# Second feed-forward product of a transformer block: two groups side by side through the seven products, sums and casts in a fixed order, token blocks of the output projection in another order

## The chip, the cores and the metric

One core of one Trainium2 chip. The number is device microseconds (us) of one execution of the whole program. A trace's own span (first to last instruction) is a little shorter than the time of the execution that was profiled.

## The reference, cut to what matters

512 tokens, model width 1024, feed-forward width 4096. After attention, mLSTM and their gates, the block ends in

```python
h = layer_norm(DEEPNORM_ALPHA * h + merged @ w_out[l], ln1_g[l], ln1_b[l])
ff = jnp.square(jax.nn.relu(h @ w_ff1[l])) @ w_ff2[l]
r = DEEPNORM_ALPHA * h + ff
r = r + jax.nn.sigmoid(r @ w_ple_gate[l]) * (p[l] @ w_ple_proj[l])
h = layer_norm(r, ln2_g[l], ln2_b[l])
```

All of it is fp32 in and out.

## The kernel before, in words

**Three matmuls for one.** Every fp32 operand is split into a rounded fp32r part and the rest (`split`, L105 to L107: ACT casts `hi`, DVE or POOL subtracts to get `lo`), and each product is hi·hi + hi·lo + lo·hi (`mm3`, L132 to L135). So each weight and each activation passes once through ACT and once through DVE or POOL before TensorE (PE) sees it.

**Seven products for eight.** Both feed-forward products are done as Winograd's variant of Strassen's: a 2x2 block product with seven block products, whose operands are sums of blocks.

**First feed-forward product** (`ff1`, L862): 16 column pieces of w_ff1, each with seven 256-wide products; `left_factors` (L786) loads a piece, POOL makes the four sums (`sums`, L793 to L796), ACT and DVE split. The other operand, `hcH`/`hcL`, holds seven combinations of the transposed first layer norm's output; `h_factors(i)` (L738) makes them of token block i: the transposes `hps` on PE, then copies, sums and splits on ACT and DVE. Blocks 0 and 1 give the plain combinations HB11 and HB21, blocks 2 and 3 all the others.

**What stands ahead of it.** The output projection (`out_projection(i, hh)`, L810: 24 matmuls for token block i and column half hh, then a DVE op adds into `r`), the first norm of each block (`first_norm`, `layer_norm` L699; its power on POOL is L705, its last two DVE operations are L715 and L716), and eight small products of the `p` input (`ple_projection`, six matmuls each, tile `ppw`).

**Second feed-forward product** (L888 to L1036). The 4096 rows of w_ff2 are four groups g. A group's activations are four blocks a11, a21, a12, a22 (two tiles `uL`, `uH`; those of groups 2 and 3 are spilled to DRAM during the first product, L932, and read back, L950), its weights four quarters B11, B12, B21, B22 of 1 MB each. The combined weights are made by DMAs that add while they write: `add` (L904) issues one from POOL's queue, onto a quarter `b` that SP's queue loaded (`load`, L898). Three quarters are loaded and four adds made per group: B12 and then B22 and then B21 onto B11's tile, B12 onto B22's tile. Each add waits until the splits of the tile's former content are done, and the next split of that tile waits for the add. POOL makes the activation sums `s` and those in `uL`, `uH` (L963 to L973). One product of one group is a step of 24 matmuls of 512 columns: PE goes through group 0's seven products, then group 1's, and so on (`steps`, 28 steps); `operands` makes a step's factors `wh`, `wl` (128x2048) and `ah`, `al` (128x1024), each with two buffers, while the step before runs. In a step all matmuls of one token half come first, with wh·ah, wl·ah, wh·al in turn. Products 0, 1 and 4 are kept in PSUM over all groups; the other four are added into `r` after every step (L1032, L1034).

**Behind it.** `load_gate` loads and splits w_ple_gate (`wpg`), `gate_inputs` transposes `r` (`rps`), `gate_product` makes eight gate products (`pg`), and `second_norm` finishes a block and stores it.

The order of instructions on each engine is set by a scheduler with a cost model of its own at build time; `tc.issue_after(x)` puts what is built inside it behind x.

Of the kernel before, what the change touches and what calls it, by code (L numbers as in the profile page):

```python
# [14 lines left out]
P = 128  # L15
# [40 lines left out]
def block_kernel(ctx: ExitStack, tc: tile.TileContext, t, out):  # L56
# [43 lines left out]
    def gtile(name, dtype=F32R):  # L100

        return gpool.tile([P, 4, S], dtype, tag="g", bufs=4, name=name)
# [593 lines left out]

    def layer_norm(pl, src, dst, g, b, done=None, pieces=2, cut=D):
# [6 lines left out]
        ve.tensor_scalar(ag[:, 2:3], ag[:, 1:2], EPS, None, op0=OP.add)  # L704
        ge.tensor_tensor(out=ag[:, 3:4], in0=ag[:, 2:3], in1=mhalf[:, 0:1], op=OP.pow)  # L705
# [26 lines left out]

    def h_factors(i):
# [25 lines left out]
        ve.tensor_sub(v3, hb[1][:, :, o], v2)  # L759
# [26 lines left out]
    def left_factors(q, half):  # L786
# [12 lines left out]
        for o, src in ((slice(0, 2), raw[:, :, :, 0:P]), (2, a22), (slice(3, 7), sums)):  # L799
            split(src, hi[:, o], lo[:, o], ge if q == order[0] and o != 2 and o.start == 0 else ve)  # L800
# [17 lines left out]
    for i in range(NT - 1):  # L818
        out_projection(i, 0)
    for i in range(NT - 1):  # L820
        out_projection(i, 1)
        first_norm(i)
        if i > 0:
            h_factors(i - 1)
# [5 lines left out]
    factors = [left_factors(order[0], half) for half in range(2)]  # L830
    first_norm(NT - 1)
    h_factors(NT - 2)
# [17 lines left out]
    for _ in range(2):  # L850
        ple_projection(*todo.pop(0))
# [10 lines left out]
    def ff1(q, acts):  # L862
# [6 lines left out]
        for half, (wh, wl) in enumerate(ws):  # L869
            for n, (a, b) in enumerate(pairs_):  # L870
                for c in range(2):
                    k = half * 2 + c
                    mm3(ps[n], wh[:, a, c], wl[:, a, c], hcH[:, b, k], hcL[:, b, k], k == 0, k == 3)
# [17 lines left out]

    ff2_rows = w_ff2.rearrange("(q j p) c -> j p q c", j=2, p=P)
# [5 lines left out]
    def load(g, w):  # L898
        if g < GROUPS:
            tl = place("b", [P, 4, 512], F32, g % 2 if w == B11 else 2 if w == B22 else 3)  # L900
            loads.append(sy.dma_start(tl, rows_of(g, w)))
            quarters.setdefault(g, {})[w] = tl
# [12 lines left out]
    def group_acts(g):  # L915
        acts[g] = gtile("uL", F32), gtile("uH", F32)
        return [a.rearrange("p (a b) (c q) -> p a (b c) q", a=2, c=2) for a in acts[g]]

    views = {}
    quarters = {}  # L920
    B = B11, B22, B21
    for n, q in enumerate(order):
        g = q // 4
        if q % 4 == 0:
            views[g] = group_acts(g)
        ff1(q, views[g])
        if n == 0:
            for a in todo:
                ple_projection(*a)
        if n in (5, 9):  # L930
            for c in range(2):
                sy.dma_start(spilled[order[n - 2] // 4][:, c], views[order[n - 2] // 4][c])  # L932
        if 6 <= n < 9:
            with tc.issue_after(loads[-1].ins):
                load(0, B[n - 6])
        if n == 9:
            f1, close_f1 = open_pool("f1", side="right")
            begun = [factor(f1, quarters[0][B11], "w", 512, hi=place("wh", [P, 4, 512], F32R, 1))]
            add(0, quarters[0][B11], B12)
        if n == 12:  # L940
            begun.append(factor(f1, views[0][0][:, 0], "a", 256))
# [4 lines left out]
    def load_acts(g):  # L946
        if g in spilled:
            views[g] = group_acts(g)
            for c in range(2):
                sy.dma_start(views[g][c], spilled[g][:, c])  # L950

    def ff2_steps(g):

        (a11, a21), (a12, a22) = ([v[:, 0], v[:, 1]] for v in views[g])
        b11, b22, b21 = (quarters[g][w] for w in B)
        fac = lambda a, b: (factor(late, b, "w", 512, 2), factor(late, a, "a", 256, 2))
        if g == 0:
            yield begun
        else:
            yield fac(a11, b11)  # L960
            add(g, b11, B12)
        s1 = late.tile([P, 4, 256], F32, tag="s1", bufs=1, name="s1")
        ge.tensor_sub(s1, a21, a22)  # L963
        load_acts(g + 1)
        yield fac(a12, b21)
        load(g + 1, B11)
        s3, s2 = a21, late.tile([P, 4, 256], F32, tag="s2", bufs=1, name="s2")
        ge.tensor_sub(s2, s1, a11)
        ge.tensor_add(a12, a12, s2)
        yield fac(s1, b11)  # L970
        add(g, b11, B22)
        load(g + 1, B21)
        ge.tensor_sub(s3, a11, s3)  # L973
        yield fac(a12, b22)
        add(g, b22, B12)
        yield fac(s2, b11)
        add(g, b11, B21)
        yield fac(s3, b22)
        load(g + 1, B22)
        yield fac(a22, b11)  # L980


    GATE_STEPS = (2, 2), (2, 6), (3, 1), (3, 3)
    steps = [(g, n) for g in range(GROUPS) for n in range(7)]
# [171 lines left out]
```

## Time and profile before

| | |
|---|---|
| runs (us) | 857.41, 854.6, 855.33; median 855.33 |
| the profiled execution's own time | 856.99 us |
| its span in the trace | 855.3 us |
| mean granted TensorE clock in it | 0.978 of full speed |
| busy: PE, DVE, ACT, POOL | 794.0, 645.9, 421.0, 380.4 us |
| matmul instructions | 4374 |
| moved by DMA | 104.16 MB |

A profile's busy time of an engine is the time in which it ran an instruction; an idle stretch is put down to what the instruction after it waited for. Matmuls are pipelined, so one that is shown as 0.40 us long is followed by the next one after 0.23 us; distances between starts tell the pace.

### The profile page before, as it was taken

The page shows a single profiled execution, that of the slowest core. Times are in us where ns is not written, and L with a number is a line of the kernel's source. Part 1 is how long each engine was busy: PE and PEld are TensorE (multiplying, and loading weights), DVE is VectorE, ACT ScalarE, POOL GpSimd, SP SyncE. Part 2 cuts the span into 40 slices and gives each one's busy share as a digit, 9 for nine tenths or more (in the row PEclk, how much of TensorE's full clock was granted, in tenths as well). Part 3 has the DMA queues.
Part 4 walks back from the last instruction along what each step waited for, and adds up shares of the span by engine and source line. Part 5 has one row for each costly group of instructions (what it writes and reads, how often), then busy time and mean ns, then how long its engine had stood idle before and what let it go on. Part 6 is the DMA issues. An engine that isn't in the chain of part 4 may idle for free.

```text
span 855.3 us, 11843 instructions
## 1 busy us (share of the span) xinstructions
PE 794.0 (93%) x4374; PEld 676.7 (79%) x4374; DVE 645.9 (76%) x1061; ACT 421.0 (49%) x687; POOL 380.4 (44%) x289
## 2 busy tenths in 40 slices
PE   8999999999999999999889999999779878788996
PEld 7787778779978888778689999999567656576785
DVE  5779999955469985767867898896858568587557
ACT  4445456677665633332546666665444344365110
POOL 4542443232344435461556678773825216123501
PEclk9999999999999999999989999999999999899999
DMA  7432224121132012670523786330595977958101
GB/s 214 129 94 73 57 68 110 50 72 54 51 98 74 26 50 85 209 223 26 183 81 106 245 234 223 114 99 1 148 252 142 185 208 168 275 130 165 50 25 74
DMA packets 86036, 104.16 MB, mean 122 GB/s; under 512 B 6229, under 2 KB 58965, under 8 KB 84698
## 3 DMA queue, kind: packets, MB, share of 16 engines
q1 hardware_dynamic: 76938, 84.53, 31.1%
q0 software_dynamic: 8448, 16.78, 11.5%
q10 hardware_dynamic: 592, 2.10, 0.7%
q8 instruction: 34, 0.56, 0.3%
q14 instruction: 24, 0.20, 0.1%
HBM read 95.00 MB, written 8.39 MB: 121 GB/s over the span
## 4 chain that ended last, share of the span: by engine, by line
PE 61%; DVE 18%; DMA 10%; issue 4%; ACT 3%; POOL 3%; SPq 0%; DVEq 0%; ACTq 0%; POOLq 0%
PE pf L134 8%; PE pf L135 8%; PE pf L133 8%; DMA b<-in_w_ff 8%; DVE wl L107 3%; PE pg L134 3%; PE pg L135 3%; PE pg L133 3%; DVE sc L329 2%; PE po L135 1%; PE po L133 1%; PE po L134 1%; DVE sc L339 1%; PE pu L133 1%; DVE al L107 1%
## 5 line engine op out<-in xcount | busy, mean ns | idle before, releaser
L133 PE MATMUL pf<-hcH,w1h 128*128 128x256 f32 x448 | 123.0, 285 | 5.3 <-DVE hcL L107 5.3
L134 PE MATMUL pf<-hcL,w1h 128*128 128x256 f32 x448 | 124.3, 283 | 0.0
L135 PE MATMUL pf<-hcH,w1l 128*128 128x256 f32 x448 | 118.7, 283 | 0.0
L134 PE MATMUL pf<-wl,ah 128*128 128x512 f32 x224 | 94.0, 420 | 21.7 <-DVE wl L107 21.7
L107 DVE TENSOR_TENSOR wl<-b,wh 128x2048 fp32r<-128x2048 f32 x28 | 82.8, 2956 | 32.3 <-ACT wh L106 32.3
L133 PE MATMUL pf<-wh,ah 128*128 128x512 f32 x224 | 90.0, 410 | 8.5 <-ACT wh L106 7.7
L135 PE MATMUL pf<-wh,al 128*128 128x512 f32 x224 | 91.8, 411 | 4.0 <-DVE al L107 4.0
L133 PEld LDWEIGHTS pf<-hcH,w1h 128*128 128x128 f32 x448 | 84.7, 191 | 5.8 <-DVE hcL L107 5.5
L134 PEld LDWEIGHTS pf<-hcL,w1h 128*128 128x128 f32 x448 | 85.5, 191 | 0.1
L135 PEld LDWEIGHTS pf<-hcH,w1l 128*128 128x128 f32 x448 | 82.1, 191 | 0.2 <-DVE w1l L107 0.2
L106 ACT CAST wh<-b 128x2048 fp32r<-128x2048 f32 x28 | 53.3, 1902 | 44.2 <-DMA b<-in_w_ff 40.3
L134 PEld LDWEIGHTS pf<-wl,ah 128*128 128x128 f32 x224 | 44.5, 199 | 37.8 <-DVE wl L107 28.6
L126 POOL TENSOR_TENSOR wgl<-wgr,wgh 128x1024 fp32r<-128x1024 f32 x16 | 39.4, 2464 | 66.7 <-ACT wgh L125 52.5
L107 DVE TENSOR_TENSOR w1l<-w1r,w1h 128x256 fp32r<-128x256 f32 (+1 forms) x62 | 49.0, 815 | 19.1 <-ACT w1h L106 19.1
L133 PEld LDWEIGHTS pf<-wh,ah 128*128 128x128 f32 x224 | 44.6, 199 | 20.8 <-ACT wh L106 9.7
L135 PEld LDWEIGHTS pf<-wh,al 128*128 128x128 f32 x224 | 44.9, 200 | 14.0 <-DVE al L107 4.9
L905 POOL DMA_DIRECT2D b<-in_w_ff x16 | 20.7, 1294 | 77.7 <-DVE wl L107 77.7
L134 PE MATMUL pg<-xL,wgh 128*128 128x512 f32 x128 | 51.5, 402 | 0.0
L133 PE MATMUL pg<-xH,wgh 128*128 128x512 f32 x128 | 51.4, 401 | 0.0
L135 PE MATMUL pg<-xH,wgl 128*128 128x512 f32 x128 | 51.3, 400 | 0.0
L106 ACT CAST w1h<-w1r 128x512 fp32r<-128x512 f32 x64 | 29.6, 511 | 42.7 <-PE pf L134 35.9
L793 POOL TENSOR_TENSOR sums<-w1r 128x256 f32<-128x256 f32 x32 | 25.2, 789 | 52.6 <-DVE w1l L107 44.4
(356 smaller groups left out, 2298.4 us busy)
## 6 DMA issues: line engine op xcount, KB each, us to landing
w1r<-in_w_ff SPq DMA_DIRECT2D x64, 256.0 KB, 3.1
b<-in_w_ff POOLq DMA_DIRECT2D x16, 1024.0 KB, 8.6
b<-in_w_ff SPq DMA_DIRECT2D x12, 1024.0 KB, 6.9
wgr<-in_w_in SPq DMA_DIRECT2D x16, 512.0 KB, 3.9
wor<-in_w_out SPq DMA_DIRECT2D x8, 512.0 KB, 3.9
wpgr<-in_w_ple_gate SPq DMA_DIRECT2D x8, 512.0 KB, 9.6
xrs<-in_x SPq DMA_DIRECT2D x4, 512.0 KB, 4.7
iqwr<-in_w_in SPq DMA_DIRECT2D x4, 512.0 KB, 4.9
```

What stands on the lines that cost most here:

```text
L106: se.copy(hi, src)
L107: (lo_eng or ve).tensor_sub(lo, src, f(hi))
L126: (lo_eng or ge).tensor_sub(lo, raw, f(hi))
L133: te.matmul(ps, sh, mh, start=first, stop=False, **kw)
L134: te.matmul(ps, sh, ml, start=False, stop=False, **kw)
L135: return te.matmul(ps, sl, mh, start=False, stop=last, **kw)
L329: ve.scalar_tensor_tensor(sc, rl, wi[:, i, h:h + 1], sc, op0=OP.mult, op1=OP.add)
L339: ve.match_replace(out=sc, in_to_replace=m8, in_values=sc, imm_value=NEG_TAKEN)
L793: ge.tensor_add(sums[:, 0], a21, a22)
L905: return ge.dma_start(out=tl, in_=rows_of(g, w), accum_op=OP.add)
```

## The change

1. **Two groups side by side.** `steps` now goes through pairs of groups (d = 0: groups 0 and 1; d = 1: groups 2 and 3), each step being one product of one group e of the pair. A product of both groups is summed in PSUM, and goes into `r` once per pair (`ff2_sums`).
2. **One add less per group.** The operand of P4, formerly B11's tile after its third add, is now B21's tile plus B11's tile after its second add, made on chip by DVE (`T4`).
3. **Activation sums from POOL to DVE**, ten of sixteen; six stay on POOL (`ON_POOL`).
4. **Fixed order.** `queued` chains all casts on ACT and all sums, splits and adds into `r` on DVE in the order of the program; PE's matmuls are chained too. Within a step the four wh·ah matmuls of a token half come first, then wh·al, and wl·ah of both halves last.
5. **Loads.** Only B11 of groups 0 and 1 is loaded during the first product; B21 and B22 of both follow at the first step of the second. B21 has tiles of its own. POOL's space for DMA descriptors goes from 8192 to 2048 bytes per partition. The raw gate weights are loaded some steps ahead of their splits.
6. **Ahead of the first product**: token blocks in the order 0, 2, 1, 3; the splits and sums of the first w_ff1 piece are put behind the last first norm's statistics and power, the splits of its sums behind the last block's combinations; all eight `ple_projection` come before the first product instead of six; and in its first piece the two products that need only blocks 0 and 1 (HB11, HB21) come first.

The core of the diff:

```diff
-        for o, src in ((slice(0, 2), raw[:, :, :, 0:P]), (2, a22), (slice(3, 7), sums)):
-            split(src, hi[:, o], lo[:, o], ge if q == order[0] and o != 2 and o.start == 0 else ve)
+        for o, src in ((slice(0, 2), raw[:, :, :, 0:P]), (2, a22)):
+            split(src, hi[:, o], lo[:, o], ge if q == order[0] and o != 2 else ve)
+        if later is None:
+            split(sums, hi[:, 3:7], lo[:, 3:7])
+        else:
+            later.append((sums, hi[:, 3:7], lo[:, 3:7]))
...
-    factors = [left_factors(order[0], half) for half in range(2)]
     first_norm(NT - 1)
-    h_factors(NT - 2)
+    later = []
+    with tc.issue_after(norm[0].ins), tc.issue_after(norm[1].ins):
+        factors = [left_factors(order[0], half, later) for half in range(2)]
+    h_factors(1)
...
     h_factors(NT - 1)
-    for _ in range(2):
+    with tc.issue_after(last_block[0].ins):
+        for a in later:
+            split(*a)
+    for _ in range(4):
         ple_projection(*todo.pop(0))
...
+        parts = [(half, n) for half in range(2) for n in range(7)]
+        if q == order[0]:
+            parts.sort(key=lambda x: x[1] not in (0, 4))
...
+    steps = [(0, P1, 0), (0, P5, 0), (0, P1, 1), (0, P2, 0), (0, P2, 1), (0, P5, 1)]
+    steps += [(0, P6, 0), (0, P3, 0), (0, P3, 1), (0, P6, 1), (0, P7, 0), (0, P7, 1)]
+    steps += [(1, P1, 0), (0, P4, 0), (0, P4, 1), (1, P1, 1), (1, P5, 0), (1, P5, 1), (1, P2, 0), (1, P2, 1)]
+    steps += [(1, P6, 0), (1, P3, 0), (1, P3, 1), (1, P6, 1), (1, P7, 0), (1, P7, 1), (1, P4, 0), (1, P4, 1)]
...
+    def factor_of(src, kind, width):
+        hi, lo = (late.tile([P, 4, width], F32R, tag=kind + x, bufs=2, name=kind + x) for x in "hl")
+        queued(se, "copy", hi, src)
+        queued(ve, "tensor_sub", lo, src, f(hi))
+        return hi, lo
...
+        if n == P1 and g > 0:
             add(g, b11, B12)
...
+        elif n == P5:
+            add(g, b11, B22)
+        elif n == P3:
+            add(g, b22, B12)
+        elif n == P7:
+            load(g + 2, B22)
+            load_acts(g + 2, 0)
+        elif n == P4:
+            load(g + 2, B21)
+            load_acts(g + 2, 1)
...
+        o, x, y = {"S1": (sums, a21, a22), "S2": (sums, sums, a11), "S3": (a21, a11, a21), "S4": (a12, a12, sums),
+                   "T4": (b21, b21, b11)}[which]
+        queued(engine, "tensor_sub" if which < "S4" else "tensor_add", o, x, y)
...
+        for s, kind in ((0, 0), (0, 1), (1, 0), (1, 1), (0, 2), (1, 2)):
+            tok = slice(s * P, (s + 1) * P)
+            def product():
+                for q in range(4):
+                    mm = te.matmul(bank(d, n, s), (al if kind == 1 else ah)[:, q, tok], (wl if kind == 2 else wh)[:, q],
+                                   start=fresh and kind == 0 and q == 0, stop=kind == 2 and q == 3, skip_group_check=True)
```

What it makes of the engines' orders, at the three places that matter. Numbers behind a name tell buffers apart.

POOL, before, from the first sum of the second product's group 0 on (`s`, `uL`, `uH`: activation sums; `DMA b`: an adding DMA):

```order
L963 TENSOR_TENSOR s_6602<-uL,uH 128x1024
L968 TENSOR_TENSOR s_6646<-s_6602,uL 128x1024
L973 TENSOR_TENSOR uL<-uL 128x1024
L969 TENSOR_TENSOR uH<-uH,s_6646 128x1024
L905 DMA b<-in_w_ff 128x4x512
L963 TENSOR_TENSOR s_6858<-uL,uH 128x1024
L973 TENSOR_TENSOR uL<-uL 128x1024
L905 DMA b<-in_w_ff 128x4x512
```

and after the change, the same stretch and on to the last add:

```order
L992 TENSOR_TENSOR uLH<-uLH 128x1024
L932 DMA b<-in_w_ff 128x4x512 x2
L990 TENSOR_TENSOR uLH<-uLH 128x1024
L932 DMA b<-in_w_ff 128x4x512 x6
L990 TENSOR_TENSOR s<-s,uLH 128x1024
L932 DMA b<-in_w_ff 128x4x512
L990 TENSOR_TENSOR uH<-uH,s 128x1024
L990 TENSOR_TENSOR uLH<-uLH 128x1024 x2
L932 DMA b<-in_w_ff 128x4x512 x2
```

POOL keeps six sums and eleven adds in this stretch; before, sixteen sums and fifteen adds stood there.

DVE, before, in the same place (`al`, `wl`: splits; `r`: a product added into the result):

```order
L107 TENSOR_TENSOR wl<-b,wh 128x2048
L107 TENSOR_TENSOR al<-uH,ah 128x1024
L107 TENSOR_TENSOR wl<-b,wh 128x2048
L107 TENSOR_TENSOR al<-s_6602,ah 128x1024
L107 TENSOR_TENSOR al<-uH,ah 128x1024
L1032 SCALAR_TENSOR_TENSOR r<-r,pf_6600 128x512
L107 TENSOR_TENSOR wl<-b,wh 128x2048
```

and after the change:

```order
L992 TENSOR_TENSOR s<-uLH,uH 128x1024
L990 TENSOR_TENSOR al<-s,ah 128x1024
L990 TENSOR_TENSOR wl<-b,wh 128x2048
L990 TENSOR_TENSOR al<-uLH,ah 128x1024
L990 TENSOR_TENSOR wl<-b,wh 128x2048
L990 TENSOR_TENSOR s<-s,uLH 128x1024
L990 TENSOR_TENSOR al<-uH,ah 128x1024
L990 TENSOR_TENSOR wl<-b,wh 128x2048
L990 TENSOR_TENSOR s<-uLH,uH 128x1024
```

The activation sums now stand in DVE's queue between the pairs of splits. From the first sum to the last `wl` of the stage this queue holds 27 `al`, 27 `wl`, 10 activation sums of 128x1024, 4 `T4` of 128x2048, 24 additions of a product (22 into `r`, 2 into `e`), 2 gate splits and 3 splits of `rps`.

POOL around the last first norm, before (`lag<-lag,mhalf` is the norm's power):

```order
L107 TENSOR_TENSOR w1l<-w1r,w1h 128x512
L795 TENSOR_TENSOR sums<-sums,w1r 128x256
L107 TENSOR_TENSOR w1l<-w1r,w1h 128x512
L795 TENSOR_TENSOR sums<-sums,w1r 128x256
L705 TENSOR_TENSOR lag<-lag,mhalf 128x1
```

and after the change:

```order
L112 TENSOR_TENSOR wp<-wpr,wp 128x1024
L712 TENSOR_TENSOR lag<-lag,mhalf 128x1
L802 TENSOR_TENSOR sums<-w1r 128x256
L803 TENSOR_TENSOR sums<-w1r 128x256
L112 TENSOR_TENSOR w1l<-w1r,w1h 128x512
```

The power now stands ahead of all work on the first w_ff1 piece.

## Rows read from the trace of the kernel before

**Rows 1.** The profile page: busy time of each engine with its share of the span; then the granted TensorE clock in tenths of full speed, over 40 slices of 21.4 us each.

```profile
PE 794.0 (93%) x4374; PEld 676.7 (79%) x4374; DVE 645.9 (76%) x1061; ACT 421.0 (49%) x687; POOL 380.4 (44%) x289
...
PEclk9999999999999999999989999999999999899999
```

**Rows 2.** The same engines over the second feed-forward product in four stretches: length, then busy us and count of PE, PEld (weight loads), DVE, ACT, POOL, then the granted clock, the DMA share and GB/s.

```profile
593.80:639.80 46.00, 36.34 (x148) 28.09 (x147) 32.84 (x20) 21.87 (x17) 28.32 (x10) 0.96 0.71 183
639.80:691.80 52.00, 43.24 (x169) 33.28 (x169) 34.68 (x23) 20.05 (x15) 16.55 (x8) 0.93 0.75 182
691.80:743.50 51.70, 41.80 (x169) 32.18 (x170) 36.61 (x23) 21.11 (x16) 19.01 (x9) 0.96 0.82 205
743.50:793.75 50.25, 44.33 (x171) 34.57 (x172) 41.78 (x32) 24.77 (x22) 18.34 (x10) 0.91 0.68 146
```

**Rows 3.** PE's groups of instructions from 595 to 800 us (the three kinds of matmul of the second product): busy us and mean ns | idle us ahead of them and what ended it.

```profile
L134 PE MATMUL pf<-wl,ah 128*128 128x512 f32 x217 | 91.2, 421 | 21.7 <-DVE wl L107 21.7
L135 PE MATMUL pf<-wh,al 128*128 128x512 f32 x217 | 89.1, 411 | 4.0 <-DVE al L107 4.0
L133 PE MATMUL pf<-wh,ah 128*128 128x512 f32 x217 | 87.3, 410 | 8.5 <-ACT wh L106 7.7 <-DVE r L1034 0.8
```

**Rows 4.** The chain of work that ended last, from 560 us on: shares by line, and two of its pieces (start us, length us, what).

```profile
by line: DMA b<-in_w_ff 21.8%; DVE wl L107 9.0%; PE pf L134 8.8%; PE pf L135 8.5%; PE pf L133 8.3%; issue 8.1%; PE pg L133 4.6%; PE pg L134 4.6%; PE pg L135 4.6%; DVE al L107 3.3%; ACT wh L106 3.2%; POOL r L1024 3.0%; POOL uL L973 1.8%; POO
...
623.93 11.21 DMA b<-in_w_ff
...
726.43 12.44 DMA b<-in_w_ff
```

**Rows 5.** PE in order of time: start us, length us, line, operation, and in brackets the idle time ahead and who ended it. The first two are of the first step, the next three of a later one, the last is the first matmul behind the second product.

```profile
594.03 0.40 PE L134 MATMUL pf<-wl,ah 128*128 128x512 f32 x1
...
598.81 0.39 PE L134 MATMUL pf<-wl,ah 128*128 128x512 f32 x1
...
609.72 0.79 PE L135 MATMUL pf<-wh,al 128*128 128x512 f32 x1 [2.41 <-DVE al L107]
610.31 0.63 PE L133 MATMUL pf<-wh,ah 128*128 128x512 f32 x1
...
612.87 0.41 PE L133 MATMUL pf<-wh,ah 128*128 128x512 f32 x1
...
806.13 0.39 PE L133 MATMUL pg<-wpg,rH 128*128 128x512 f32 x1
```

**Rows 6.** Who waited for whom from 594 to 806 us: total us, times, longest us.

```profile
ACT wh L106 <- DMA b<-in_w_ff: 40.0, 11, 6.7
...
DVE wl L107 <- ACT wh L106: 32.3, 16, 5.0
...
DVE al L107 <- ACT ah L106: 4.5, 7, 2.7
```

**Rows 7.** DVE in order of time, the same columns as rows 5: one `wl` beside work on POOL, then `wl`, `r`, `al`, `wl` with POOL idle.

```profile
601.87 4.49 DVE L107 TENSOR_TENSOR wl<-b,wh 128x2048 fp32r<-128x2048 f32 x1
...
637.18 2.29 DVE L107 TENSOR_TENSOR wl<-b,wh 128x2048 fp32r<-128x2048 f32 x1 [2.85 <-ACT wh L106]
639.39 0.68 DVE L1034 TENSOR_TENSOR r<-r,pf 128x512 f32<-128x512 f32 x1
639.99 1.22 DVE L107 TENSOR_TENSOR al<-uL,ah 128x1024 fp32r<-128x1024 f32 x1
641.12 2.29 DVE L107 TENSOR_TENSOR wl<-b,wh 128x2048 fp32r<-128x2048 f32 x1
```

**Rows 8.** POOL: an activation sum and the six additions of `e` into `r` in order of time (columns as above); then the adding DMAs' issues over the whole run (ns min/median/max).

```profile
648.91 2.39 POOL L969 TENSOR_TENSOR uH<-uH,s 128x1024 f32<-128x1024 f32 x1 [3.94 <-DVE al L107]
...
788.95 11.53 POOL L1024 TENSOR_TENSOR r<-r,e 128x512 f32<-128x512 f32 x6
...
L905 POOL DMA_DIRECT2D b<-in_w_ff x16: 1255/1282/1483, 498.9 to 779.7; - x16
```

**Rows 9.** Single microseconds: columns as in rows 2. In the first, two loads of 1 MB each run alone; in the second, one adding DMA.

```profile
604.00:605.00 1.00, 1.00 (x6) 0.83 (x5) 1.00 (x1) 0.00 (x0) 1.00 (x2) 1.00 1.05 393
...
615.00:616.00 1.00, 1.00 (x6) 0.84 (x5) 1.00 (x1) 0.00 (x0) 0.64 (x1) 1.00 1.15 211
```

**Rows 10.** Ahead of the first product, in order of time (columns as in rows 5): POOL's two splits and the power of the last norm, DVE's last norm operations, PE's transposes of the last block and its wait, and the return of the full pace.

```profile
415.75 1.48 POOL L107 TENSOR_TENSOR w1l<-w1r,w1h 128x512 fp32r<-128x512 f32 x1
...
420.72 0.54 POOL L705 TENSOR_TENSOR lag<-lag,mhalf 128x1 f32<-128x1 f32 x1
...
422.69 1.41 DVE L716 SCALAR_TENSOR_TENSOR r<-r,lag,ln_brow 128x512 f32<-128x512 f32 x2
...
425.81 2.35 DVE L107 TENSOR_TENSOR w1l<-sums,w1h 128x1024 fp32r<-128x1024 f32 x2
...
424.85 0.63 PE L139 MATMUL hps<-ident,r 128*128 128x128 f32 x4 [0.62 <-DVE hcL L107]
430.74 0.58 PE L133 MATMUL pf<-hcH,w1h 128*128 128x256 f32 x1 [5.27 <-DVE hcL L107]
...
435.39 0.28 PE L134 MATMUL pf<-hcL,w1h 128*128 128x256 f32 x1
```

**Rows 11.** ACT's two casts of a step in order of time (columns as in rows 5).

```profile
635.24 1.91 ACT L106 CAST wh<-b 128x2048 fp32r<-128x2048 f32 x1 [5.59 <-DMA b<-in_w_ff]
637.05 1.04 ACT L106 CAST ah<-uL 128x1024 fp32r<-128x1024 f32 x1
```

More of the change, by code (lines that the diff above doesn't have):

```diff
@@ L944, in block_kernel, with load_acts @@
     late, close_late = open_pool("late", side="left")
-    def load_acts(g):
+    def load_acts(g, c):
         if g in spilled:
[L948 to L958, printed above, removed]
-        else:
-            yield fac(a11, b11)
-            add(g, b11, B12)
[L962 to L980, printed above, removed]
@@ new lines, in factor_of, with parts_of, operands @@
+    def factor_of(src, kind, width):
[3 more added lines that the diff above has]
+        return hi, lo
+    def parts_of(d, e):
+        g = 2 * d + e
+        return ([views[g, 0][:, k] for k in range(2)] + [views[g, 1][:, k] for k in range(2)]
+                + [quarters.get((g, w)) for w in (B11, B22, B21)] + [both.get(g)])
+    def operands(d, n, e):
+        g = 2 * d + e
+        if n == P1:
+            both[g] = late.tile([P, 4, 256], F32, tag=f"s{e}", bufs=1, name="s")
+        a11, a21, a12, a22, b11, b22, b21, sums = parts_of(d, e)
+        a, b = {P1: (a11, b11), P2: (a12, b21), P3: (a12, b22), P4: (a22, b21), P5: (sums, b11), P6: (sums, b11),
+                P7: (a21, b22)}[n]
+        if n == P1 and g == 0:
+            ops = begun
+        else:
+            fa = factor_of(a, "a", 256)
+            ops = factor_of(b, "w", 512), fa
+        if n == P1 and g > 0:
+            add(g, b11, B12)
+        elif n == P5:
[8 more added lines that the diff above has]
+            load_acts(g + 2, 1)
+        return ops
@@ L987, in block_kernel @@
+    banks, before = {}, []
+    for n in (P1, P6):
         for s in range(2):
[L988 removed]
+            banks[n, s] = misc("pf2")
     for s in range(2):
[L990 to L1012 removed]
+        banks[P5, s] = banks[P3, s] = acc("pf2")
@@ L1073, in block_kernel @@
             e16 = tail.tile([P, 2, 512], F32, name="e16")
+            for w in (B21, B22):
+                for g in range(2):
+                    load(g, w)
+        if k and steps[k - 1][2]:
+            ff2_sums(*steps[k - 1][:2])
+        if (d, n, e) in AHEAD:
+            sum_of(*AHEAD[d, n, e])
+        if (d, n, e) in ON_POOL:
+            sum_of(*ON_POOL[d, n, e], ge)
         nxt = operands(*steps[k + 1]) if k + 1 < len(steps) else None
-        if last and n == 0:
-            pws = [gtile("pw", F32).rearrange("p (a b) c -> p a (b c)", a=2) for _ in range(2)]
+        if (d, n, e) in BEHIND:
+            sum_of(*BEHIND[d, n, e])
+        if (d, n, e) == (1, P7, 1):
+            pws = [gtile("pw", F32, 2 * j).rearrange("p (a b) c -> p a (b c)", a=2) for j in range(2)]
             for j in range(2):
```

224 lines of the change are left out of this document (130 added, 94 removed).

## The prediction

> **What bounds the kernel now.** I read the page first: PE is busy 93% of the span, and its granted clock falls off in the last third [rows 1]. So any gain lies where PE idles or is slowed. Next the stretches. The second feed-forward product runs 27 of its 28 steps from 593.80 to 793.75 us; the four stretches add up to 199.95 us, in which PE is busy 165.71 [rows 2]. A step is 24 matmuls. At full pace one follows the other after 0.228 us (21 of them from 594.03 to 598.81 [rows 5]); beside heavy traffic I have seen 0.233, so I take 0.230, 5.52 us a step. 27 steps would need 149.0 us and take 7.41 us each: **50.9 us are lost**. Idle time is 199.95 - 165.71 = 34.2 of them. The other 16.7 are slow pace: after an idle of 2.41 us the six matmuls from 610.31 to 612.87 follow each other after 0.427 us, the 1.2 GHz level instead of 2.4 [rows 5].
>
> PE's own rows say what it waits for: the split `wl` of the weights (21.7 us), the cast `wh` (7.7), the split `al` (4.0) [rows 3]. These are not slow engines: ACT waits 40.0 us for DMA and DVE 32.3 us for ACT's `wh` [rows 6]. The chain names the root, the adding DMAs, 21.8% of it, single ones at 11.2 and 12.4 us [rows 4]. Within a group each add starts after one product's splits and is needed one or two products later. POOL has a part in it: a `wl` beside POOL's sums takes 4.49 us, with POOL idle 2.29 [rows 7].
>
> A second loss lies at the start of the first product. PE waits 0.62 and 5.27 us, and up to 435.39 it runs at half pace; that is some 22 matmuls of 256 columns at 0.21 instead of 0.12 us, 2.0 us more. Together **7.9 us** [rows 10].
>
> **The change, part by part: the adds.** With two groups interleaved, the splits of one content of a tile and the cast of the next are two to five steps apart, 11.0 to 27.6 us, against 11.2 to 12.4 us for the adds that end the waits now [rows 4]. Only group 3's B12 add (steps 15 to 17, counted from 0) has no more than two steps: up to 1.4 us late. At the start the four loads of B21 and B22 leave when the first step has done with `wh`, 16 x 0.230 = 3.7 us into it. A load costs the DMA engines 2.67 us (1.05 MB at 393 GB/s), an add 5.0 (at 211 GB/s) [rows 9]. Four loads and two adds are 20.7 us of work; group 1's first add is wanted at 4 x 5.52 + 1.3 = 23.4 us, with 3.7 + 20.7 = 24.4 us if it came last. I take 1.5 us for all late landings; below, nothing. In the whole stage DMA work falls: 11 adds instead of 15, 55 us, with some 48 for 18 MB of loads, in about 160. So it does not bound.
>
> **DVE and POOL together.** POOL's sum takes 2.39 us [rows 8], DVE starts the next operation after 1.13 us for an operation of that size (`al`), 2.21 for a `wl`, 0.60 for an `r` [rows 7]. DVE's queue in the stage: 27 x 3.34 = 90.2 (`al` and `wl`), 10 sums x 1.13 = 11.3, 4 `T4` x 2.21 = 8.8, 24 additions x 0.60 = 14.4, gate and `rps` splits 2 x 1.13 + 3 x 0.60 = 4.1: 128.8 us. POOL: 6 sums x 2.39 = 14.3, two gate splits 4.8, six additions of `e` into `r`, 7.2 (half of 2.39 each; they take 11.53 beside DVE now [rows 8]): 26.3 us. If the two never overlap, as the 4.49 us suggest, they need 155.1 us against PE's 154.6 for 28 steps. So they hardly bound on average, but they do where work is bunched. The order puts `wl`'s matmuls last, so a late `wl` has 3.7 us of grace. Steps 17 to 21 hold 23.6 us on DVE and four POOL sums, 9.6: 33.2 against 27.6 + 3.7, **1.9 us** over. Steps 24 to 26 hold 18.2 on DVE and 9.7 on POOL: 27.9 against 16.6 + 3.7, 7.6 over, of which the 18 gate matmuls that now stand inside the last step cover 4.1: **3.5 us**. Pace: these waits come in pieces of 1 to 2 us, two stretches at half pace at about 1.5 us, **3 us**. Left of the 50.9: 1.9 + 3.5 + 1.5 + 3.0 = 9.9; gained **41.0**. Bounds: 4 left (only the bunched ends) and 27 (half of today's loss).
>
> A rule that speaks against this: the issue of an add takes POOL 1255 to 1483 ns in all 16 cases, busy DVE or not [rows 8], so I charge nothing for more DVE work beside POOL's issues. The Trainium skill, SBUF — State Buffer, section "SBUF: two separate sides", warns that a DVE operation in a two-port mode keeps POOL from writing an add's descriptors. By that rule each of the 11 adds could leave one DVE operation later; by the row none does. It is rival 3.
>
> **Ahead of the first product.** POOL's norm power runs at 420.72, behind splits and sums of the first weight piece from 415.75 on [rows 10]; now it stands ahead of them. But DVE has more to do before it: block 2's seven combination operations come earlier in place of block 1's two, some 5 x 0.68 = 3.4 us [rows 7], with a few us of gaps to hide them. I therefore leave the last block's transposes at about 424 us. What fills PE behind them is new: 12 `ppw` matmuls at 0.23 and 12 more of the two products that need blocks 0 and 1 alone at 0.12, 4.2 us, up to 428.3. DVE's chain for block 3 no longer has the two splits of sums (2.35 us [rows 10]) at its head; they stand behind its last combination. The first operand PE then lacks comes at about 429.4 (behind the transposes a copy of 0.6 and seven operations of 0.68); the wait is 1.1, and later operands cost another 1.3: 2.4 of the 7.9 us stay, **5.5 gained** (2 if the wait still halves the pace, 7 if it goes). The token order itself, the loads moved out of the first product and the placed tiles I cost at nothing: PE has no gap there that they could close or open. The smaller descriptor space costs nothing as long as not over three adds are under way; the order keeps it at two.
>
> **Sum.** 856.99 (the profiled execution) - 41.0 - 5.5 = 810.5. That execution lies 1.7 above the median 855.33, so against the runs: **809 us**. Range: 855.3 - 46.9 - 7 = 801 to 855.3 - 24 - 2 = 829.
>
> **Rivals.**
> 1. *DVE's queue becomes the bound.* Its order is fixed now, so a waiting operation holds all behind it. `ah` is in use up to the last matmul of its step and has two buffers; its next cast (1.04 us) starts only with the next step, and `wh`'s (1.91) behind it [rows 11]. DVE would so stand 1.04 for `al` and 1.91 - 1.13 = 0.78 more for `wl`, unless a sum or an addition fills the gap, which it does in most steps. Today it waits 32.3 + 4.5 us, 1.36 per step [rows 6]. With half of that, 28 x (155.1/28 + 0.68) = 174 us: 20 lost, 5 more for pace, **824 us**. For: both engines' work fills the stage. Against: the fillers.
> 2. *Landings stay late.* Loads, spill reads and adds bunch at the start and where the pair changes (step 12). Four waits of 4 us and four stretches at half pace of 2: 24 more on some of the above, **827 us**. For: adds of 12 us; against: the two to five steps.
> 3. *Descriptors held up by DVE.* Two adds have no slack; 2 x 2.3 late and twice 2 us at half pace: **818 us**. Against: 1483 ns at most.
> 4. *Slower.* The mechanism of rival 1 at full length: DVE stands 2.06 us or more in every step. That is the turning point: 155.1/28 = 5.54, and 7.41 + 5.5/28 - 5.54 = 2.07. At 2.3, 28 x (7.84 - 7.41) - 5.5 = 6.5 more: **862 us**. For: 1.04 + 0.78 = 1.8 of it is there, and the signals between the engines could add the rest; against: it needs every gap unfilled.
> 5. *The stage gains nothing* and the front only its lower bound, 2 us: within the noise. The orders show that the change does what it says, so this has little.
>
> **How the numbers follow.** Forecast 0.60; rivals 1 to 3: 0.18, 0.12, 0.04; rival 4: 0.04; rival 5: 0.02. Faster by over 0.3% (about what a measurement of this kernel can tell from no change) is the first four: 0.94; same 0.02; slower 0.04. The range holds forecast, rivals 1 to 3 at their prices and the bounds, and leaves out their ends, some 0.1 to 0.15.
>
> **What would show it.** In the changed profile PE's idle time between the first and the last step falls from 34 to under 10 us, the stage from 7.41 to about 5.9 us a step; ACT's waits for `b` DMAs nearly vanish; DVE is busy about 90% of the stage; PE's waits name `wl` or `al`, mostly in steps 17 to 21 and at the end; the wait of 5.27 us ahead of the first product shrinks below 3. I am wrong if ACT still waits for `b` over 15 us (rival 2), or DVE shows over 20 us of waits for ACT (rivals 1 and 4).

## The result, and the profile after

The changed kernel takes **827.88 us** (median; 826.58 to 833.12), the kernel before 856.33 beside it on the same chip: 0.968 of the time, 95% interval 0.963 to 0.973. So it is 28.5 us faster, and 19 us slower than forecast; the time lies within the range, near its upper end. The profiled execution took 826.58 us.

The page answers to [rows 1]. PE has lost 8.5 us of busy time, most of it half pace that has gone (the matmuls are the same 4374); the granted clock still falls off at three places in the last third and in the last slice.

```profile
PE 785.5 (95%) x4374; PEld 674.2 (82%) x4374; DVE 651.2 (79%) x1063; ACT 420.3 (51%) x687; POOL 350.2 (42%) x275
...
PEclk9999999999999999999999999999998989989998
```

The second feed-forward product in four stretches (columns as in [rows 2]): its 28 steps begin at 590.33 us, 3.5 earlier than before, and its last eight matmuls start from 772.91 on. Three stretches hold 4.5 to 6 us of idle time each, at a clock of 0.93; the last has none. In the second the DMA engines are full.

```profile
590.33:640.33 50.00, 44.49 (x187) 36.02 (x186) 38.48 (x27) 24.57 (x19) 10.01 (x6) 0.93 0.65 161
640.33:690.33 50.00, 45.47 (x189) 37.03 (x188) 37.08 (x26) 22.19 (x17) 3.85 (x3) 0.93 0.97 295
690.33:740.33 50.00, 44.03 (x177) 34.59 (x176) 43.41 (x25) 23.61 (x18) 19.59 (x8) 0.93 0.50 92
740.33:772.91 32.58, 32.58 (x152) 26.69 (x151) 31.47 (x23) 17.11 (x16) 22.28 (x10) 1.00 0.51 145
```

PE in order of time (columns as in [rows 5]): 14.0 of the 16.0 us of idle time are three waits for a cast `wh`. Behind each of them PE runs at half pace: four matmuls take 1.87 us from 623.50 to 625.37 and 0.91 from 628.42 to 629.33.

```profile
623.50 2.08 PE L1070 MATMUL pf<-wh,ah 128*128 128x512 f32 x4 [5.33 <-ACT wh L990]
625.37 1.91 PE L1070 MATMUL pf<-wh,al 128*128 128x512 f32 x4
627.08 1.51 PE L1070 MATMUL pf<-wh,ah 128*128 128x512 f32 x4
628.42 1.07 PE L1070 MATMUL pf<-wh,al 128*128 128x512 f32 x4
629.33 1.98 PE L1070 MATMUL pf<-wl,ah 128*128 128x512 f32 x8
...
663.03 2.07 PE L1070 MATMUL pf<-wh,ah 128*128 128x512 f32 x4 [4.53 <-ACT wh L990]
...
727.68 2.08 PE L1070 MATMUL pf<-wh,ah 128*128 128x512 f32 x4 [4.17 <-ACT wh L990]
```

They stand at steps 5, 11 and 21 (counted from 0). Who waited for whom over the stage answers to [rows 6]: ACT's waits for `b` have fallen from 40.0 to 14.6 us, two single ones, and those are the first two waits of PE.

```profile
DVE wl L990 <- ACT wh L990: 20.1, 15, 7.6
...
PE pf L1070 <- ACT wh L990: 15.7, 6, 5.3
...
ACT wh L990 <- DMA b<-in_w_ff: 14.6, 2, 7.7
```

**Waits 1 and 2.** POOL's adding DMAs in order of time (start us, length of the issue, idle time ahead):

```profile
598.75 1.33 POOL L932 DMA_DIRECT2D b<-in_w_ff  x1 [4.10 <-DVE wl L990]
613.29 1.27 POOL L932 DMA_DIRECT2D b<-in_w_ff  x1 [13.22 <-DVE wl L990]
...
637.18 1.26 POOL L932 DMA_DIRECT2D b<-in_w_ff  x1 [9.69 <-PE pf L1070]
646.82 1.29 POOL L932 DMA_DIRECT2D b<-in_w_ff  x1 [8.37 <-DVE al L990]
```

The second add is the one that step 5 needs. What it must wait for, the split of its tile, starts on DVE at 599.43 and takes 2.29 us; it could leave at 602 and leaves at 613.29.

```profile
599.43 2.29 DVE L990 TENSOR_TENSOR wl<-b,wh 128x2048 fp32r<-128x2048 f32 x1
```

The trace puts the late issue down to a `wl` which had long been done, so the true releaser is another. The DMA engines tell which: they are full until 613.3, the moment at which the first add has landed (14.3 us after it left).

```profile
596.00:613.30 17.30, 17.19 (x76) 14.24 (x77) 15.73 (x10) 9.03 (x8) 1.33 (x2) 1.00 1.04 321
613.30:614.80 1.50, 1.50 (x8) 1.26 (x7) 1.25 (x2) 0.56 (x1) 1.50 (x2) 1.00 0.30 112
```

The add at 646.82, which step 11 needs, likewise leaves 4 us behind its split and only when the one of 637.18 has landed; then it takes 14.19 us beside loads and spill reads.

```profile
613.29 8.17 DMA b<-in_w_ff
...
646.82 14.19 DMA b<-in_w_ff
```

Of the eleven adds of the stage five leave 0.26 to 0.32 us after the one ahead has landed, and none leaves before that. So the adds go one at a time now. The kernel before issues some 4 us apart (experiment 2).

**Wait 3.** DVE and POOL around it: three sums on POOL from 711.53 to 723.6, and three DVE operations in that time that take 3.4 to 4.5 us instead of 1.22, 2.29 and 1.22. The last, `uH`, is what the cast for step 21 waits for.

```profile
713.50 3.44 DVE L990 TENSOR_TENSOR al<-s,ah 128x1024 fp32r<-128x1024 f32 x1
716.86 4.48 DVE L990 TENSOR_TENSOR wl<-b,wh 128x2048 fp32r<-128x2048 f32 x1
721.26 3.41 DVE L990 TENSOR_TENSOR uH<-uH,s 128x1024 f32<-128x1024 f32 x1
```

```profile
711.53 4.33 POOL L990 TENSOR_TENSOR uH<-uH,s 128x1024 f32<-128x1024 f32 x1 [3.16 <-issue]
715.80 7.78 POOL L990 TENSOR_TENSOR uLH<-uLH 128x1024 f32<-128x1024 f32 x2
```

**Ahead of the first product** (answers to [rows 10]): the wait of 5.27 us is now one of 2.48 and one of 0.46, and half pace still follows it.

```profile
428.79 0.39 PE L138 MATMUL pf<-hcH,w1h 128*128 128x256 f32 x1 [2.48 <-DVE hcL L112]
...
431.24 0.80 PE L138 MATMUL pf<-hcH,w1h 128*128 128x256 f32 x2 [0.46 <-ACT hcH L111]
```

```profile
429.00:439.00 10.00, 9.54 (x69) 9.24 (x69) 6.51 (x11) 3.20 (x8) 6.50 (x8) 0.83 0.29 92
```

### The profile page after: what moved, and what is told of

The parts are those of the page before. It is cut to its first block, busy times and chain, and to the rows that moved or that the text cites. A ratio compares the mean times of both kernels' runs of the same rounds, so it can differ in the third digit from the quotient of the medians.

```text
span 824.9 us, 11806 instructions
## 1 busy us (share of the span) xinstructions
PE 785.5 (95%) x4374; PEld 674.2 (82%) x4374; DVE 651.2 (79%) x1063; ACT 420.3 (51%) x687; POOL 350.2 (42%) x275
## 4 chain that ended last, share of the span: by engine, by line
PE 66%; DVE 20%; ACT 5%; DMA 4%; issue 4%; POOL 2%; SPq 0%; DVEq 0%; ACTq 0%; POOLq 0%
PE pf L1070 11%; PE pf L138 6%; PE pf L139 6%; PE pf L140 6%; DMA b<-in_w_ff 3%; PE pg L139 2%; PE pg L140 2%; PE pg L138 2%; DVE sc L344 2%; DVE m L343 2%; DVE wl L990 2%; ACT wh L990 2%; DVE sc L334 2%; PE po L140 2%; PE po L138 2%
## 5 line engine op out<-in xcount | busy, mean ns | idle before, releaser
L990 DVE TENSOR_TENSOR wl<-b,wh 128x2048 fp32r<-128x2048 f32 x27 | 67.9, 2517 | 20.1 <-ACT wh L990 20.1
L1070 PE MATMUL pf<-wh,ah 128*128 128x512 f32 x224 | 65.7, 418 | 15.7 <-ACT wh L990 15.7
L1070 PE MATMUL pf<-wh,al 128*128 128x512 f32 x224 | 63.3, 406 | 0.0
L932 POOL DMA_DIRECT2D b<-in_w_ff x12 | 15.7, 1305 | 110.9 <-DVE wl L990 72.0
L990 ACT CAST wh<-b 128x2048 fp32r<-128x2048 f32 x27 | 51.3, 1901 | 16.6 <-DMA b<-in_w_ff 14.6
L1070 PE MATMUL pf<-wl,ah 128*128 128x512 f32 x224 | 55.8, 391 | 0.3 <-DVE wl L990 0.2
L1070 PEld LDWEIGHTS pf<-wh,al 128*128 128x128 f32 x224 | 44.5, 199 | 10.2 <-DVE al L990 0.3
L1070 PEld LDWEIGHTS pf<-wl,ah 128*128 128x128 f32 x224 | 41.8, 188 | 9.9 <-DVE wl L990 1.2
L112 DVE TENSOR_TENSOR w1l<-sums,w1h 128x1024 fp32r<-128x1024 f32 x32 | 47.2, 1479 | 1.4 <-ACT w1h L111 1.4
```

What stands on the lines that cost most here:

```text
L112: (lo_eng or ve).tensor_sub(lo, src, f(hi))
L932: return ge.dma_start(out=tl, in_=rows_of(g, w), accum_op=OP.add)
L990: order_of[engine] = getattr(engine, op)(*args, **kw)
L1070: mm = te.matmul(bank(d, n, s), (al if kind == 1 else ah)[:, q, tok], (wl if kind == 2 else wh)[:, q], start=fresh and kind == 0 and q == ...
```

## The experiments

Two theories for waits 1 and 2. A: POOL's space for descriptors, cut from 8192 to 2048 bytes, holds one add, so the next is issued when it has landed. B: the adds wait for an engine, and are late through traffic alone. For wait 3, C: DVE and POOL do not work at the same time; D: it is DVE's queue whatever POOL does. Ratios are to the kernel before, run beside each.

**1. More space.**

```diff
-dynamic_dma_scratch_size=2048
+dynamic_dma_scratch_size=4096
```

> The changed kernel (827.88 us) with 4096 instead of 2048 bytes per partition for POOL's DMA descriptors, nothing else. Theory A (the small space holds one add's descriptors, so POOL issues an add only when the one before has landed): the second add of the stage leaves near 602.6 instead of 613.29 us, the fifth near 643.6 instead of 646.82; four loads, half a load of the gate and two adds are some 22 us of DMA work from 596 us on, so the second add lands near 618 instead of 621.5: PE's wait of 5.33 us falls to about 2, that of 4.53 (step 11) below 1, and the half pace behind the latter goes: 8 to 10 us less, about 819 us. Theory B (the issues are held by the operation they wait for, and the adds are late because of the traffic alone): issue times and waits stay, 828 us.

Measured: **817.03 us** (ratio 0.956, 0.953 to 0.958), 10.9 less, with the order of the instructions unchanged on every engine. The second add leaves at 601.88, the fifth at 641.41, each right behind its split, and wait 2 is gone.

```profile
598.55 1.30 POOL L932 DMA_DIRECT2D b<-in_w_ff  x1 [4.04 <-DVE wl L990]
601.88 1.26 POOL L932 DMA_DIRECT2D b<-in_w_ff  x1 [2.03 <-DVE wl L990]
```

PE's waits over 1 us that are left are these, the second of them new (step 17, group 3's add of B12, which the prediction had named as the tightest):

```profile
622.05 1.27 PE L1070 MATMUL pf<-wh,ah 128*128 128x512 f32 x4 [4.03 <-ACT wh L990]
...
693.89 1.41 PE L1070 MATMUL pf<-wh,ah 128*128 128x512 f32 x4 [3.50 <-ACT wh L990]
...
720.17 1.20 PE L1070 MATMUL pf<-wh,ah 128*128 128x512 f32 x4 [1.98 <-ACT wh L990]
```

A holds, and B alone is out. But the first wait shrank by 1.3 us only: now both adds share the DMA engines with four loads; the first lands at 612.9 and the second at 620.0, against 613.0 and 621.5 with the small space.

```profile
601.88 18.14 DMA b<-in_w_ff
```

Wait 3 has changed with no edit of its own: it is 1.98 us instead of 4.17; where the late add of step 17 is gone as well, it is 4.17 again (experiment 9).

**2. The kernel before with the small space.**

```diff
-dynamic_dma_scratch_size=8192
+dynamic_dma_scratch_size=2048
```

> The kernel before (856.33 us) with 2048 instead of 8192 bytes per partition for descriptors, nothing else. Theory A: adds that leave 4.2 and 3.9 us apart now (661.42 and 665.66, 766.23 and 770.17) move 7 us or more apart, each not before the one ahead of it has landed, and since the chain runs over the adds the kernel gets 4 to 10 us slower, 860 to 866 us. Theory B: nothing moves, 856 us.

Measured: **868.59 us** (1.016, 1.013 to 1.019), 13.3 slower than before, more than expected. The two adds that left 4.2 us apart now leave 8.8 apart:

```profile
663.73 1.31 POOL L905 DMA_DIRECT2D b<-in_w_ff  x1
672.50 1.27 POOL L905 DMA_DIRECT2D b<-in_w_ff  x1 [7.45 <-issue]
```

The space acts by itself, on either order of the work.

**3. Space between the two.** The same line with 3072.

> The changed kernel with 3072 bytes for descriptors, nothing else (2048: 827.88 us, 4096: 817.03). If an add needs room for all its descriptors before it is issued and 2048 hold one add, 3072 hold one as well: the second add leaves at 613 us, 828 us. If room is handed back piece by piece, the second add starts to leave when a part of the first has been worked off: near 605 to 608 us, 820 to 825 us.

Measured: **817.34 us** (0.957, 0.954 to 0.959), the same as with 4096; the second add leaves at 601.95. Neither guess was right: 3072 bytes already hold two adds.

**4. Adds in two halves, with 2048 bytes.**

```diff
-        return ge.dma_start(out=tl, in_=rows_of(g, w), accum_op=OP.add)
+        for h in (slice(0, 2), slice(2, 4)):
+            ge.dma_start(out=tl[:, h], in_=rows_of(g, w)[:, h], accum_op=OP.add)
```

> The changed kernel, 2048 bytes for descriptors, with every adding DMA cut in two of half a megabyte each. If the space is handed back when a DMA has landed and 2048 bytes hold two halves, the first half of the second add leaves when the first half of the first add has landed, near 606 us instead of 613.3, and each add starts some 3 us earlier behind another: 821 to 824 us. If the second issue of 1.3 us on POOL and a second landing cost more than that, or a half also waits for the whole of what is ahead: 828 to 832 us.

Measured: **817.00 us** (0.956, 0.953 to 0.958), better than expected and as good as more space.

```profile
598.13 2.43 POOL L933 DMA_DIRECT2D b<-in_w_ff  x2 [4.03 <-DVE wl L991]
601.52 1.19 POOL L933 DMA_DIRECT2D b<-in_w_ff  x1 [0.97 <-DVE wl L991]
608.53 1.19 POOL L933 DMA_DIRECT2D b<-in_w_ff  x1 [5.82 <-issue]
```

The third half leaves 3.4 us behind the first, and no half in this trace lands in under 5.4 us, as the view of all its halves shows (shortest, median, longest); the fourth leaves at 608.53, 0.3 us after the first has landed.

```profile
DMA to landing us min/median/max: 5.4/8.7/14.9
```

So 2048 bytes hold one and a half adds of 1 MB and not two.

**5. Loads out of the way of the first adds** (2048 bytes).

```diff
-            for w in (B21, B22):
-                for g in range(2):
-                    load(g, w)
+            for g in range(2):
+                load(g, B21)
...
+        if k in (3, 5):
+            load(k // 4, B22, by_act=True)
```

`by_act` queues the load on ACT, here behind its casts for step k + 1.

> The changed kernel with the loads of B22 of groups 0 and 1 issued by ACT behind its casts for steps 4 and 6 (near 610 and 621 us) instead of by SP at the first step. If the four loads in front of the first two adds make the wait of 5.33 us: the first add lands near 608 instead of 613.3, the second leaves then and lands near 615, and the wait falls to about 1.5 us; with part of the half pace behind it 4 to 6 us less, about 823 us. Rival: B22 is then late itself for steps 7 and 8, waits of 2 to 4 us there, 826 us or more.

Measured: **824.04 us** (0.964, 0.962 to 0.966), 3.8 less. The second add leaves 8.9 us behind the first (609.41 after 600.48) instead of 14.5, and wait 1 falls to 2.34; B22 is nowhere waited for.

**6. Both.** The edits of 1 and 5.

> 4096 bytes for descriptors (817.03 us by itself) and, on top, the loads of B22 of groups 0 and 1 issued by ACT behind its casts for steps 4 and 6. Theory A with traffic: only two loads, half a load of the gate and two adds are left in front of the cast that waited until 620.1: 5.3 + 1.3 + 10 = 16.7 us of DMA work from 596 on, done near 613, when the cast wants it; the wait of 4.03 us at 622.05 and the half pace behind it go, 5 to 6 us less, about 811.5 us. Rival: two adds under way together are slow by themselves, whatever the loads do; the wait stays over 2.5 us, 815 us or more.

Measured: **813.44 us** (0.951, 0.948 to 0.955). The wait at step 5 is gone; those of 3.08 (step 17) and 1.98 stay. Wait 1 had two causes, then: the space, which put the adds one behind the other, and the loads, which made the first of them long. The two profiled executions differ more in the stage than in the time: from the second product's first matmul to the span's end it is 218.0 us instead of 224.3 in experiment 1, 6.3 less, but that product begins 3.7 later (593.86 instead of 590.18), at a place that the edit does not touch.

**7. POOL's last sums later** (2048 bytes).

```diff
-               (1, P6, 0): ["S3", 1, 0], (1, P3, 0): ["S3", 1, 1]}
+               (1, P3, 0): ["S3", 1, 0], (1, P3, 1): ["S3", 1, 1]}
```

Each is also put behind the add of B12 onto B22 that was built last.

> The changed kernel with POOL's last two activation sums (S3 of groups 2 and 3) put behind the two adds of B12 onto B22 that follow them now. Theory C (the wait of 4.17 us at 727.68 comes of DVE and POOL working at the same time: al 3.44, wl 4.48 and uH 3.41 us against 1.22, 2.29 and 1.22 with POOL idle): the wait falls below 1 and the half pace behind it goes, 5 to 7 us less, about 822 us. Rival D (the sums only meet other DVE work two steps on, which is as full): 2 us less at most, the wait moves to steps 22 to 25.

Measured: **826.41 us** (0.967, 0.964 to 0.970), no difference that can be told. Wait 3 falls to 0.24, but a wait of 2.61 comes two steps on, at 743.88. An add is also late at step 17 (2.36); that need not come of the sums, as experiment 12 leaves them alone and has 2.17 there. At the later place the sums meet another `wl`:

```profile
729.56 5.25 DVE L992 TENSOR_TENSOR wl<-b,wh 128x2048 fp32r<-128x2048 f32 x1
```

```profile
729.75 2.91 POOL L992 TENSOR_TENSOR uLH<-uLH 128x1024 f32<-128x1024 f32 x1
```

5.25 is 2.29, a `wl` alone, and 2.96 more, and the sum takes 2.91: DVE stands still for all of POOL's operation. C holds for the single operations, D for the time. The Trainium skill, SBUF — State Buffer, section "SBUF: two separate sides", says that the port pair these two engines share is an exclusive lock, kept for a whole instruction, and not a split of the bandwidth; these two rows agree. That it is the `wl` that stands, though it starts 0.19 us ahead of the sum, they leave open.

**8. The last four sums on DVE** (4096 bytes).

```diff
-    ON_POOL = {(0, P5, 1): ["S3", 0, 0], (0, P3, 0): ["S3", 0, 1], (1, P2, 0): ["S2", 1, 1], (1, P2, 1): ["S4", 1, 1],
-               (1, P6, 0): ["S3", 1, 0], (1, P3, 0): ["S3", 1, 1]}
+              (1, P2, 0): ["S2", 1, 1], (1, P6, 0): ["S4", 1, 1], (1, P3, 1): ["S3", 1, 0], (1, P6, 1): ["S3", 1, 1]}
+    ON_POOL = {(0, P5, 1): ["S3", 0, 0], (0, P3, 0): ["S3", 0, 1]}
```

> 4096 bytes for descriptors (817.03 us by itself) and, on top, the last four activation sums that POOL kept (S2 and S4 of group 3, S3 of groups 2 and 3) on DVE, behind the splits of steps 18, 20, 22 and 23. Theory C (DVE and POOL do not work at the same time: a sum costs 2.39 us on POOL and 1.13 on DVE, and either stops DVE for that long): wl 4.10, al 3.43 and wl 4.48 us at 704 to 716 us return to 2.29, 1.22 and 2.29, PE's waits of 0.33 and 1.98 us there go, 2 to 3 us less, about 814.5 us. Rival (DVE's queue becomes the bound once it has all sums): waits on wl or wh of 1 us and more in steps 19 to 25, 817 us or more.

Measured: **817.08 us** (0.956, 0.954 to 0.959) against 817.03. The waits of 0.33 and 1.98 go, and three others come behind step 23: 0.61, 1.17 and 1.27 us. The rival is right about the time; of its waits only that of 0.61 lies in the steps it named, and that of 1.17 is put down to POOL's additions into `r`, not to DVE.

**9. All loads of B22 late** (4096 bytes), sums as the change has them.

```diff
-            load(g + 2, B22)
...
+        if k in (3, 5, 17, 18):
+            load({3: 0, 5: 1, 17: 2, 18: 3}[k], B22, by_act=True)
```

> 4096 bytes for descriptors and the loads of B22 of all four groups by ACT, with all sums where the change has them (four of group 2 and 3 on POOL). With these four on DVE as well the kernel took 806.96 us, and with 4096 bytes alone they were worth nothing (817.08 against 817.03). If the loads alone remove the waits for adds, and the sums are worth nothing here either: 807 us, with waits of 0.33 and 1.98 us behind steps 19 and 20. If theory C holds for the time and not only for the single operations: the waits of 2.3 us and the half pace behind them count, 809 to 810 us.

Measured: **810.56 us** (0.948, 0.946 to 0.950). No wait for an add is left. Wait 3 is back with its 4.17 us, at 711.91, and half pace behind it: without the late add at step 17 the sums meet the same DVE operations as in the changed kernel.

**10. Space, late loads and sums on DVE**: the edits of 1, 8 and 9 together.

> 4096 bytes for descriptors, the loads of B22 of all four groups issued by ACT (behind the casts for steps 4, 6, 18 and 19), and the last four sums of POOL on DVE. The DMA engines are full from 646 to 694 us with 4096 bytes alone; B22 of groups 2 and 3 are 5.3 us of that and wanted only at steps 21 and 22, so the add that lands at 691.9 would land near 686.6, before its cast wants it (689.2): the wait of 3.50 us at 693.89 goes too. Sum against 817.03: 5.5 (second add), 2.5 (sums), 5 (this wait and its half pace): about 804 us. If the traffic is only moved on to the adds at 687 and 697 (groups 2 and 3, B22 onto B11), a wait of 2 to 4 us comes back in steps 20 to 23: 808 to 810 us.

Measured: **806.96 us** (0.944, 0.942 to 0.946), the fastest here and 20.9 us below the changed kernel. Over the stage PE waits 4.7 us, and the clock is 1.00 throughout.

```profile
PE pf L1072 <- ACT wh L993: 3.5, 5, 1.3
PE rps L144 <- POOL r L1108: 1.2, 1, 1.2
```

```profile
590.00:754.00 164.00, 159.29 (x704) 130.01 (x704) 145.32 (x104) 89.03 (x70) 42.01 (x22) 1.00 0.73 189
```

Against 9, the sums on DVE are worth 3.6 us now, where in 8 they were worth nothing: in 8 PE was waiting for adds ahead of the place.

**11. POOL's additions into `r` on DVE too.**

```diff
-                    (ge.tensor_sub if c else ge.tensor_add)(rs, rs, e16[:, s])
+                    deferred.append(("tensor_sub" if c else "tensor_add", rs, rs, e16[:, s]))
```

DVE does three of them behind the splits of step 25 and three behind those of step 26.

> The version of 806.96 us (4096 bytes, four late loads, four sums on DVE) with the six additions of e into r on DVE too, three behind the splits of step 25 and three behind those of step 26. On POOL they run for 15.64 us beside DVE, whose al, wl and T4 take 2.31, 3.38 and 3.38 us there against 1.22, 2.29 and 2.29. Theory C: DVE is spared some 6 us of these and gets 3.6 us of additions, PE's waits of 1.17 and 1.27 us go: 804.5 us. Rival: the additions stand in front of splits that are wanted at once (steps 26 and 27): 807 us or more.

Measured: **813.07 us** (0.951, 0.949 to 0.953), 6 us slower than 10. PE waits 2.51 us for an `al` and 2.82 for a `wh` at steps 26 and 27. Time on DVE was spared, but in front of what PE wanted next. Of the 8.3 us between the two profiled executions 5.1 lie behind the start of the second product; the other 3.2 lie ahead of it (it begins at 593.03 instead of 589.83), where the order on PE, DVE and POOL is the same in both.

**12. The front undone** (2048 bytes): token order, splits, small products and product order ahead of the first product as before.

```diff
-    for i in (0, 2, 1):
+    for i in range(NT - 1):
...
-    with tc.issue_after(norm[0].ins), tc.issue_after(norm[1].ins):
-        factors = [left_factors(order[0], half, later) for half in range(2)]
+    factors = [left_factors(order[0], half) for half in range(2)]
...
-        if q == order[0]:
-            parts.sort(key=lambda x: x[1] not in (0, 4))
```

> The changed kernel (827.88 us) with the part ahead of the first product undone: token blocks 0, 1, 2, 3, the first w_ff1 piece split where it was, six small products of p ahead of the first product and two behind its first piece, products in the old order. From the last output projection to the first matmul of the second product the kernel before takes 187.16 us (406.64 to 593.80), the changed one 184.02 (406.31 to 590.33). If the parts only add up, that distance returns to 187 us and PE's wait of 5.27 us with it: 3.1 us more, 831 us. Rival, by the forecast's own term of 5.5 us: 833.5 us. If the front has no share that lasts: 828 us.

Measured: **830.19 us** (0.971, 0.969 to 0.973; the changed kernel 0.968, 0.963 to 0.973), 2.3 slower in the medians, which the intervals do not separate. In the trace the wait of 5.27 is back, and from the last output projection to the second product it takes 185.7 us (409.15 to 594.84): 1.7 more than with the change, 1.5 less than before. One trace does not settle it: over the eleven traces here with the new front the same distance goes from 182.7 to 185.7 us (median 183.3), and the three with the old one have 187.2, 187.2 and 185.7.

## Why the prediction was right or wrong, point by point

Losses are taken from the distances between PE's starts, less 0.23 us for each matmul.

- **What bounds the kernel**: right. The adds were the root; with their slack ACT's waits for `b` fell from 40.0 to 14.6 us, and the distance from the second product's first matmul to the span's end shrank from 261.5 to 234.6 us, by 26.9 where 41.0 were forecast. Of the stage 25.3 us are still lost, not 9.9: PE idles for 16.0 us, not under 10, and a step takes 6.5 us, not 5.9.
- **All late landings, 1.5 us: here it failed.** The two waits cost 5.47 + 4.66 us and the half pace behind them 2.16 + 2.83 (which stands in the term for pace as well), 15.1 in all. The step that was wrong is the last sentence on the front: "The smaller descriptor space costs nothing as long as not over three adds are under way; the order keeps it at two." No row of the trace bore the three. 2048 bytes hold fewer than two (experiment 4), and the order puts two under way. Alone this is 10.9 us of the time (experiment 1). In the traces it is 10.2 behind the start of the stage: the second wait goes with its half pace (7.5), 1.8 of the first and 5.0 of wait 3 go too, and 4.0 come at step 17. What is left of the first wait is the four loads in front of the first two adds (experiment 6: it goes, 6.3 us less in the stage, 3.6 in the time). So the estimate of 24.4 us of DMA work against 23.4 of room was too short as well: with space the second add lands 29.8 us after the stage begins (590.18 to 620.02), 5.4 later. It took the rates of single microseconds in which loads or an add ran alone, and left out the half load of the gate that runs beside them; which of the two weighs more is not shown.
- **Bunched steps 17 to 21, 1.9 us**: the place was right and the size was not. Waits of 0.83, 0.65 and 0.17 us and wait 3 come to about 7 us, and half pace to another 2.9. The sum of 33.2 us of work against 31.3 took DVE and POOL as free to use every gap; three sums of POOL in a row stopped DVE in front of the one operation that was wanted. Steps 24 to 26, **3.5 us**, cost nothing: the last stretch has no idle time.
- **Pace, 3.0 us**: 7.9 measured, three stretches of 2.2 to 2.9 us, one behind each wait over 4 us. It was put at 1.5 us a stretch.
- **The front, 5.5 us**: 3.5 by the start of the stage, of which the edits there make some 2 to 4, as far as the traces tell (experiment 12). The waits of 2.48 + 0.46 are near the 2.4 that were forecast; the half pace behind them, 10 us at 0.83, was not in the sum. It is not always there: over the eleven traces with this front those ten microseconds were granted 0.66 to 1.00, with 4096 bytes alone 1.00.
- **Sum**: 15.4 us more lost in the stage and 2.0 less gained ahead of it are 17.4, against the 16.1 by which the profiled execution missed 810.5; 1.3 came back elsewhere.
- **Rivals.** Landings stay late (827 us, "four waits of 4 us and four stretches at half pace") gave the time and two of the three waits, though more through the space than through the traffic it named (experiments 1 and 5). Its test, ACT's waits for `b` over 15 us, missed it by 0.4. DVE's queue as the bound is out for this kernel, though its sign was there: DVE waits 20.1 us for `wh` and 11.4 for `ah`, against a mark of 20. Most of that is the shadow of the late casts (7.3 and 9.8 in experiment 10), and DVE is busy 82% of the stage, not 90%; in experiment 11, at 88%, PE does wait 2.51 us for an `al` of it. Descriptors held up by DVE: out, with room the adds leave within 0.4 us of what they wait for. No run shows that DVE's operations here are of the two-port kind that the rule of this rival is about.
- Where the three causes are removed (space, loads, sums) the same order of steps gives 806.96 us. So the slack of two to five steps was as wide as claimed; what was missing was the room to use it. That this is near the 809 of the forecast is luck: the loads and four sums stand elsewhere there.

## What to carry to other kernels

A resource that a change makes smaller and that the old trace never shows short is an unknown cost: bound it from both sides, "every transfer waits for the one before" being the one end, instead of setting it to nothing. When an issue leaves late and the trace names a releaser that was long done, look at what ended at that very moment, here the landing of the transfer ahead. Slack in the order is worth only what the transfers may run side by side, and loads wanted six steps later do not belong in front of an add wanted in three.

## What the runs showed of the hardware that was not expected

- Descriptor space for POOL's DMAs: 2048 bytes per partition hold one and a half adds of 128x4x512 fp32 and not two, 3072 hold two; halving each DMA helped as much as more space (817.00 and 817.03 us). The Trainium skill, DMA: Bandwidth & Descriptors, section "SWDGE vs HWDGE vs iDMA", says that GpSimd writes these descriptors to rings in SBUF which the DMA engines drain; that an issue waits when they are full is what these runs add.
- The same space is worth 13.3 us to the kernel before, in which adds left 4 us apart.
- A DVE operation on two tiles in SBUF that meets one of POOL's sums is longer by all of the latter (5.25 instead of 2.29 us beside a sum of 2.91). The additions of a product from PSUM are not: in the changed kernel four of them follow each other after 0.6 us beside POOL's split of a gate weight, as they do with POOL idle [rows 7].

```profile
763.92 2.47 DVE L990 TENSOR_TENSOR r<-r,pf 128x512 f32<-128x512 f32 x4
```

```profile
763.92 4.77 POOL L990 TENSOR_TENSOR wpg<-wpgr,wpg 128x1024 fp32r<-128x1024 f32 x2
```

- The same wait of 2.48 us ahead of the first product was followed by half pace in one execution (0.83) and by full pace in another (1.00, in experiment 1). The second product begins between 589.8 and 593.9 us for the same front, so a single pair of traces can be 4 us apart for that alone.
